# Latent attention in a hybrid decoder trunk: rotated query's products first, values per token in places of their own, latents' scaling with priority

## The chip, the cores and the metric

The kernel runs on one core of a Trainium2 chip. The metric is the device time of one execution in microseconds (us). Engines go by the profile's names: PE is TensorE's matrix multiply, PEld its weight load, DVE is VectorE, ACT is ScalarE, POOL is GpSimd, SP is SyncE, which only issues transfers here. Each engine takes its instructions in the order in which the program has them, and waits at an instruction until the results that it needs are there.

## The reference

Two layers of a decoder trunk, for one sequence of 512 tokens with 1024 channels, in float32. Each layer normalises its input, projects it, and runs three branches side by side: a Mamba-2 state-space branch (SSD), multi-head latent attention (MLA), and a gated DeltaNet. Each branch is projected and gated, their sum goes through an output projection, and a feed-forward block of width 4096 follows. The change touches the MLA branch:

```python
q = (rmsnorm(cq, q_norm_g) @ w_uq).reshape(Bsz, S, H, MLA_NOPE + MLA_ROPE)
q_nope, q_pe = jnp.split(q, [MLA_NOPE], axis=-1)
q_pe = apply_rope(q_pe, cos[:, :, None, :], sin[:, :, None, :])
kv = (rmsnorm(ckv, kv_norm_g) @ w_ukv).reshape(Bsz, S, H, MLA_NOPE + MLA_V)
k_nope, v = jnp.split(kv, [MLA_NOPE], axis=-1)
k_pe = apply_rope(k_rope, cos, sin)
```

Here cq (512 wide) and ckv (256 wide) are the two latents, H is 8 heads, a head has 128 plain and 64 rotated columns for queries and keys and 128 for values. Scores are the sum of the plain and the rotated product, causal, followed by softmax and the product with the values.

## The kernel before

**Precision.** Each float32 product is made of three faster ones: both operands are split into a high part (a copy on ACT, L159 for weights, L256 and L260 for activations) and a low part (a subtraction on DVE, L160, L257, L261), and PE adds high x high, low x high and high x low (L181 to L183). So before PE can use a tile, ACT and then DVE have to pass over it. Weights come through SP's queue into two raw buffers, are split in pieces of 512 columns, and the splits (tiles whi and wlo) go through a ring of buffers: a cast waits until PE is done with the piece that held its buffer.

**Banks.** PE writes to eight accumulation banks of 512 columns. The program takes them from groups: acc (products, four), sm (scores, transposes, short sums, three) and yt (attention outputs, one). A new tile of a group waits for the last reader of the tile that had the bank.

**A layer's order around MLA.** The input projections of cq, ckv and the rotated key columns come first. Function latent then normalises each latent: per block of 128 tokens ACT squares and sums it (L491), DVE and POOL make the reciprocal root (L264 on DVE, a power on POOL, L265), DVE scales the four blocks (L495), PE transposes them (L500), and split_gain (L260 on ACT for the tile cqh or ckh, L261 on DVE for cql or ckl) splits the transposed tile, times the gain. It is called for cq, then for ck.

Then comes a loop over four pairs of heads (hp). For each pair:

- q products (L181 to L183): weights of 512 rows by 384 columns, in two loads of two 128-row tiles each, split at L552 to L555. The 384 columns are three tiles: head 0, head 1 and the rotated columns of both (pp).
- qh and ql of both heads (L568, L569); qp, the scaled copy of pp (L575); its rotation in rope: four transfers on ACT's queue that swap halves (L513), and three DVE passes with the cosine and sine tables (L515 to L517); a swap of the two heads' halves by two more transfers (L580); and copies into qps and qpl, the high and low parts (L584 to L586).
- k products for both heads, split into kh and kl, with a raised priority; then V for both heads, per block of 128 tokens, split into vh and vl (L257 by way of ev).
- for each head: scores per block of 128 tokens (L607 to L612; L610 and L611 are the rotated part), a row maximum (L616, DVE), an exponential (L619, ACT), a reciprocal and a scaling (L620, L621, DVE); transposes of the probabilities (L629), their split (tiles mix and pt), and the product with V (L645 to L647) into yt; its split gives the head's output y.

**Who orders the instructions.** The program text is not the order on the engines. A list scheduler places instructions by their priority, which follows the text unless a block raises it (tc.high_priority), as soon as it estimates that their inputs are ready. It so fills PE's waits with products of the next head pair, and at the end of MLA with the SSD branch's first input projections (w_in weights, tiles acc<-xh,whi), whose convolution (L661 to L665, tile cva) follows on ACT and DVE.

## Time and profile before

| what | value |
|---|---|
| median of 3 runs | 2356.81 us (2356.48 to 2356.88) |
| the profiled execution | 2355.78 us |
| its span, first to last instruction | 2354.0 us |
| granted PE clock | 0.999 |
| busy: PE, DVE, ACT | 98%, 68%, 49% |
| MLA in layer 0 | about 57 to 196 us |
| MLA in layer 1 | about 1224 to 1361 us |

A row of a timeline gives start, length, engine, line, operation, output tile and input tiles, shape, and how many instructions were put together; in square brackets stands how long the engine was idle before the row, and what released it. The view of waits sums such idle times by line and releaser: total, times, longest. A row of the windows view gives a stretch, its length, the busy time of PE, PEld, DVE, ACT and POOL with their instruction counts, then the granted PE clock, the share of the transfer engines and GB/s. The view of transfers gives for each group the queue, the count, the size of one, and the time from issue to landing.

### The profile page before, as it was taken

How to read it: one execution, taken by the hardware profiler on the slowest of the kernel's cores; microseconds unless marked ns; L12 is line 12 of the kernel's file. 1: busy time of each engine (PE TensorE's matmuls, PEld its weight loads, DVE VectorE, ACT ScalarE, POOL GpSimd, SP SyncE). 2: the span in 40 equal slices, each digit the busy share in tenths (PEclk: the TensorE clock that was granted, in tenths of full speed). 3: DMA queues.
4: the chain of work that ended last, by engine and by line, in shares of the span. 5: the costliest groups of instructions: out<-in, count | busy, mean ns of one | idle time of the engine just before them, and what ended most of it. 6: DMA issues, size and time to landing. Idle time of an engine off the chain costs nothing.

```text
span 2354.0 us, 32092 instructions
## 1 busy us (share of the span) xinstructions
PE 2312.0 (98%) x11972; PEld 1901.6 (81%) x11972; DVE 1610.0 (68%) x3184; ACT 1155.4 (49%) x2305; POOL 62.5 (3%) x84
## 2 busy tenths in 40 slices
PE   8999999999999999999999999999999999999998
PEld 7778788888887888888887787888888878888886
DVE  6776756775675468667767767667756645677668
ACT  6655434533454345545656553444335534455545
POOL 0000000000000000000000000000000000000000
PEclk9999999999999999999999999999999999999999
DMA  4222232252222443233132222223422224333231
GB/s 136 85 64 71 70 92 72 76 148 72 72 63 72 138 151 106 72 126 116 44 100 79 72 72 71 91 67 104 117 81 63 63 81 159 128 109 107 90 108 45
DMA packets 194172, 215.16 MB, mean 91 GB/s; under 512 B 32352, under 2 KB 153696, under 8 KB 194016
## 3 DMA queue, kind: packets, MB, share of 16 engines
q1 hardware_dynamic: 190496, 207.87, 27.9%
q10 hardware_dynamic: 3520, 5.25, 0.9%
q8 instruction: 94, 1.54, 0.3%
q14 instruction: 62, 0.51, 0.1%
HBM read 200.50 MB, written 7.34 MB: 88 GB/s over the span
## 4 chain that ended last, share of the span: by engine, by line
PE 81%; issue 9%; DVE 5%; DMA 2%; ACT 1%; POOL 1%; SPq 0%; ACTq 0%; DVEq 0%; POOLq 0%
PE acc L181 20%; PE acc L183 20%; PE acc L182 20%; PE sm L181 2%; PE sm L183 2%; PE sm L182 2%; DVE wlo L160 1%; PE sm L629 1%; PE yt L182 1%; PE yt L183 1%; PE yt L181 1%; PE sm L984 1%; PE sm L724 1%; PE sm L965 1%; DMA mix<-mix 1%
## 5 line engine op out<-in xcount | busy, mean ns | idle before, releaser
L160 DVE TENSOR_TENSOR wlo<-wraw,whi 128x512 fp32r<-128x512 f32 x552 | 378.6, 689 | 399.3 <-ACT whi L159 392.5
L159 ACT CAST whi<-wraw 128x512 fp32r<-128x512 f32 x552 | 342.0, 621 | 628.1 <-PE acc L182 417.2
L181 PE MATMUL acc<-xh,whi 128*128 128x512 f32 (+1 forms) x1184 | 462.2, 391 | 2.2 <-DVE vl L257 2.2
L183 PE MATMUL acc<-xh,wlo 128*128 128x512 f32 (+1 forms) x1184 | 459.3, 388 | 0.0
L182 PE MATMUL acc<-xl,whi 128*128 128x512 f32 (+1 forms) x1184 | 459.0, 388 | 0.0
L181 PEld LDWEIGHTS acc<-xh,whi 128*128 128x128 f32 x1184 | 222.8, 189 | 44.3 <-DVE vl L257 2.8
L182 PEld LDWEIGHTS acc<-xl,whi 128*128 128x128 f32 x1184 | 223.0, 188 | 42.7 <-issue 1.0
L183 PEld LDWEIGHTS acc<-xh,wlo 128*128 128x128 f32 x1184 | 222.9, 188 | 42.1 <-issue 0.5
L181 PE MATMUL acc<-yh,whi 128*128 128x512 f32 x384 | 153.1, 402 | 0.0
L182 PE MATMUL acc<-yl,whi 128*128 128x512 f32 x384 | 152.4, 397 | 0.0
L183 PE MATMUL acc<-yh,wlo 128*128 128x512 f32 x384 | 151.4, 394 | 0.0
L183 PE MATMUL acc<-whi,xl 128*128 128x512 f32 (+1 forms) x384 | 144.1, 376 | 0.0
L181 PE MATMUL acc<-whi,xh 128*128 128x512 f32 (+1 forms) x384 | 143.4, 375 | 0.0
L182 PE MATMUL acc<-wlo,xh 128*128 128x512 f32 (+1 forms) x384 | 143.1, 373 | 0.0
L665 DVE SCALAR_TENSOR_TENSOR cva<-acc,pc,cva 128x511 f32<-128x511 f32 (+2 forms) x168 | 120.2, 743 | 16.7 <-ACT cva L661 9.5
L159 ACT CAST whi<-wr 128x512 fp32r<-128x512 f32 x128 | 79.5, 621 | 68.2 <-PE acc L183 29.0
L183 PE MATMUL acc<-whi,yl 128*128 128x512 f32 x256 | 99.7, 390 | 0.0
L181 PE MATMUL acc<-whi,yh 128*128 128x512 f32 x256 | 99.7, 389 | 0.0
L182 PE MATMUL acc<-wlo,yh 128*128 128x512 f32 x256 | 99.6, 389 | 0.0
L160 DVE TENSOR_TENSOR wlo<-wr,whi 128x512 fp32r<-128x512 f32 x128 | 86.0, 688 | 12.4 <-ACT whi L159 11.7
L181 PEld LDWEIGHTS acc<-yh,whi 128*128 128x128 f32 x384 | 71.6, 188 | 16.9 <-ACT yh L260 2.3
L182 PEld LDWEIGHTS acc<-yl,whi 128*128 128x128 f32 x384 | 72.2, 188 | 16.0 <-issue 1.9
(382 smaller groups left out, 4601.7 us busy)
## 6 DMA issues: line engine op xcount, KB each, us to landing
wraw<-in_w_in_dram SPq DMA_DIRECT2D x148, 512.0 KB, 3.4
wraw<-in_w_up_dram SPq DMA_DIRECT2D x64, 512.0 KB, 3.6
wr<-in_w_down_dram SPq DMA_DIRECT2D x32, 1024.0 KB, 4.9
wraw<-in_w_mla_out_dram SPq DMA_DIRECT2D x16, 512.0 KB, 3.3
wraw<-in_w_ssd_out_dram SPq DMA_DIRECT2D x16, 512.0 KB, 3.3
wraw<-in_w_gdn_out_dram SPq DMA_DIRECT2D x16, 512.0 KB, 3.3
wraw<-in_w_out_dram SPq DMA_DIRECT2D x16, 512.0 KB, 3.5
wraw<-in_mla_w_uq_dram SPq DMA_DIRECT2D x16, 384.0 KB, 3.3
```

Source lines behind the costliest of these rows:

```text
L159: act.copy(hi, raw)
L160: dve.tensor_tensor(lo, raw, f32(hi), ALU.subtract)
L181: pe.matmul(o, ah, bh, start=start, stop=False, skip_group_check=more)
L182: pe.matmul(o, ah, bl, start=False, stop=False, skip_group_check=more)
L183: pe.matmul(o, al, bh, start=False, stop=stop, skip_group_check=more)
L629: pe.transpose(ps[:, n : n + P], pn[t][:, kb * P : (kb + 1) * P], ident)
L665: dve.scalar_tensor_tensor(acc[:, d:], ps[:, : S - d], taps_[3 - d], acc[:, d:], ALU.mult, ALU.add)
L724: pe.matmul(py[:, h * 64 : (h + 1) * 64], e2[h // 4][:, h % 4, :], xd[:, h * 64 : (h + 1) * 64], start=True, stop=True)
L965: pe.matmul(pw[:, h * P : (h + 1) * P], Y[:, h, :], r[:, h * P : (h + 1) * P], start=True, stop=True)
L984: pe.matmul(po[:, h * P : (h + 1) * P], pt_[:, h, :], vn[:, h * P : (h + 1) * P], start=True, stop=True)
```

## The change

Three edits in MLA, in both layers; the arithmetic stays as it is.

1. In latent, squares, reciprocal root and scaling stand in a high-priority block, and the fourth tile's transposes go to a bank of the yt group, not of sm.
2. The q products of a pair go in two rounds of two weight tiles; in each round the rotated columns come first, then head 1, then head 0.
3. The values' tiles lie in places of their own for every other pair: pair 1 in the place that outputs y6 and y7 take later, pair 3 in the places of cq's tiles 0 and 1, pairs 0 and 2 in the two vh and vl buffers. V goes through dense_T with a hook: the products of one token block are finished and split before those of the next, where before all four blocks shared each weight piece and were split at the end. The outputs y are claimed one by one when they are made.

```diff
@@ latent
-            for t in range(T):
-                jk = mk(ml, [P, width], F32, "pn3", 2)
-                act.activation(jk, tok[t], AF.Square, accum_out=ss[:, t : t + 1])
-            rs = mk(sp, [P, T], F32, "lrs")
-            rsq(rs, ss, 1.0 / width, EPS)
-            for t in range(T):
-                dve.tensor_scalar(tok[t], tok[t], rs[:, t : t + 1], None, ALU.mult)
+            with tc.high_priority():
+                for t in range(T):
+                    jk = mk(ml, [P, width], F32, "pn3", 2)
+                    act.activation(jk, tok[t], AF.Square, accum_out=ss[:, t : t + 1])
+                rs = mk(sp, [P, T], F32, "lrs")
+                rsq(rs, ss, 1.0 / width, EPS)
+                for t in range(T):
+                    dve.tensor_scalar(tok[t], tok[t], rs[:, t : t + 1], None, ALU.mult)
...
-                ps = sm_bank()
+                ps = y_bank() if k == 3 else sm_bank()
@@ the loop over head pairs
-        yh, yl = hilo_tags(lp, "y")
+        yh, yl = [None] * KD, [None] * KD
...
-            *pq, pp = dense_F(q_weights(), tiles(384), 512, cqh, cql)
+            pss = [acc_bank() for _ in range(3)]
+            gen = q_weights()
+            for k0 in (0, 2):
+                two = [next(gen) for _ in range(2)]
+                for ps, c in reversed(list(zip(pss, tiles(384)))):
+                    for k, wh, wl in two:
+                        mm3(ps, wh[:, 0, c], wl[:, 0, c], cqh[k], cql[k], k == 0, k == 3)
+            *pq, pp = pss
...
-            vs = [[mk(ml, [P, T, P], F32R, nm, 2) for nm in ("vh", "vl")] for _ in range(2)]
+            vs = []
+            for j in range(2):
+                if hp % 2 == 0:
+                    v2 = [mk(ml, [P, S], F32R, nm, 2) for nm in ("vh", "vl")]
+                elif hp == 1:
+                    v2 = [mk(lp, [P, S], F32R, f"y{e}{6 + j}") for e in "hl"]
+                else:
+                    v2 = [mk(ml, [P, S], F32R, f"cq{e}{j}") for e in "hl"]
+                vs.append([x.rearrange("p (t n) -> p t n", t=T) for x in v2])
...
-            dense_T(wkv, 256, 256, ckh, ckl, ev, lambda w: w.rearrange("p (h n) -> p h n", h=2)[:, :, P:])
+            vcols = lambda w: w.rearrange("p (h n) -> p h n", h=2)[:, :, P:]
+            dense_T(wkv, 256, 256, ckh, ckl, ev, vcols, hook=lambda t: None)
...
                         pe.matmul(o, v_l, th[:, c : c + w], start=False, stop=kb == T - 1)
+                yh[2 * hp + j], yl[2 * hp + j] = (mk(lp, [P, S], F32R, f"y{e}{2 * hp + j}") for e in "hl")
                 split_act(yh[2 * hp + j], yl[2 * hp + j], po)
```

## The prediction

> **What bounds the kernel now.** I read the page first (busy time, chain), then what TensorE (PE) waits for over the whole run, then the timelines of PE, DVE and ACT around each of those waits.

> ```profile
> PE 2312.0 (98%) x11972; PEld 1901.6 (81%) x11972; DVE 1610.0 (68%) x3184; ACT 1155.4 (49%) x2305; POOL 62.5 (3%) x84
> ...
> PE 81%; issue 9%; DVE 5%; DMA 2%; ACT 1%; POOL 1%; SPq 0%; ACTq 0%; DVEq 0%; POOLq 0%
> ```

> PE is busy for 2312.0 of 2354.0 us, and the change neither adds nor removes a matmul. So it can win only PE's idle time inside the two attention stages, and lose by making new idle time there. The view of PE's waits (us in total, times, longest) has these rows of those stages:

> ```profile
> PE acc L181 <- DVE vl L257: 3.6, 4, 1.1
> PE sm L610 <- ACT qps L586: 3.2, 4, 1.4
> ...
> PE sm L500 <- DVE mix L495: 2.0, 2, 1.0
> ...
> PE sm L500 <- DVE cql L261: 1.2, 1, 1.2
> ...
> PE acc L181 <- ACT cqh L260: 0.6, 2, 0.3
> ...
> PE yt L646 <- DVE mix L257: 0.5, 2, 0.2
> ```

> These sum to 11.1 us in 15 waits. A product is shown longer than the distance to its successor:

> ```profile
> 67.10 0.40 PE L182 MATMUL acc<-cql,whi 128*128 128x512 f32 x1
> 67.33 0.40 PE L183 MATMUL acc<-cqh,wlo 128*128 128x512 f32 x1
> ```

> Starts lie 0.23 apart, each lasts 0.40 (0.39 at most other rows), so a shown idle of i costs i + 0.16. The 15 waits cost 11.1 + 2.4 = **13.5 us**: all that can be won, 0.57%. Below, every new wait is counted in the same measure, from the start that PE could have had to the start that it gets, and set against these 13.5.

> **The change part by part.** Both programs' instruction order per engine is known, with what each instruction waits for; only their times are not. DVE, ACT and PE take their instructions in that order, so I put durations of before on the changed order.

> **1. Latents with priority.** PE, then ACT and DVE, layer 0:

> ```profile
> 56.90 1.47 PE L500 MATMUL sm<-ct,mix 128*128 128x128 f32 x12
> 58.67 0.98 PE L181 MATMUL acc<-cqh,whi 128*128 128x512 f32 x3 [0.30 <-ACT cqh L260]
> 60.86 0.66 PE L500 MATMUL sm<-ct,mix 128*128 128x128 f32 x4 [1.21 <-DVE cql L261]
> ...
> 64.79 0.63 PE L500 MATMUL sm<-ct,mix 128*128 128x128 f32 x4 [0.97 <-DVE mix L495]
> ```
> ```profile
> 57.93 1.85 ACT L260 ACTIVATE cqh<-sm,pc 128x512 fp32r<-128x512 f32 x3
> 59.65 0.43 ACT L491 ACTIVATE pn<-mix 128x256 f32<-128x256 f32 x1
> ```
> ```profile
> 59.96 0.19 DVE L415 TENSOR_SCALAR dtq<-spl 128x64 f32<-128x64 f32 x1
> 60.06 2.06 DVE L261 SCALAR_TENSOR_TENSOR cql<-sm,pc,cqh 128x512 fp32r<-128x512 f32 x3
> ...
> 62.94 0.16 DVE L264 TENSOR_SCALAR lrs<-lss 128x4 f32<-128x4 f32 x1
> 64.29 0.62 DVE L495 TENSOR_SCALAR mix<-mix,lrs 128x256 f32<-128x256 f32 x2 [1.19 <-POOL lrs L265]
> ```

> Before, the four cql come first, then ck's lrs, its power on POOL (1.35 us from lrs to the first scaling) and four scalings, 0.31 each. In the changed order lrs and the four scalings stand ahead of the four cql. The scalings wait on POOL, and all cql are queued behind them; the ck transposes wait for cql 0, whose bank they reuse. The fourth cq transposes have a bank of their own, so 16 run at once: 56.90 + 16 x 0.12 = 58.86. ACT does ck's fourth square ahead of cqh 0 (0.5 us), so PE starts the first three products at about 59.25: 0.4 lost. It would reach the ck transposes at 59.93. DVE is full until 60.1 in either kernel; lrs 60.1, scalings from 61.4, cql 0 from 62.65 to 63.4: **3.45 lost**. In layer 1:

> ```profile
> 1225.28 0.96 PE L181 MATMUL acc<-cqh,whi 128*128 128x512 f32 x3 [0.29 <-ACT cqh L260]
> ...
> 1230.01 0.63 PE L500 MATMUL sm<-ct,mix 128*128 128x128 f32 x4 [0.98 <-DVE mix L495]
> ```
> ```profile
> 1224.54 1.84 ACT L260 ACTIVATE cqh<-sm,pc 128x512 fp32r<-128x512 f32 x3
> ```

> DVE is idle there when the square ends, 0.6 behind the old start of cqh 0: lrs 1225.15, scalings from 1226.5, cql 0 done 1228.5, PE ready at 1226.5: 2.0, and 0.4 again. After 0.4 + 3.45 + 0.4 + 2.0 = 6.25, before (0.30 + 1.21 + 0.97 + 0.29 + 0.98) + 5 x 0.16 = 4.55: **+1.7**. Were POOL's 1.35 nothing, the new waits would be 6.25 - 2.7 = 3.55; with as much DVE work more ahead of them as the four scalings are, some 8.

> [...] PE's longest idle time in this trace is at the start:

> ```profile
> 8.98 0.90 PE L296 MATMUL sm<-ct,xr 128*128 128x128 f32 x3 [8.98 <-DVE xr L291]
> ```
> ```profile
> 9.00:12.00 3.00, 2.70 (x12) 2.27 (x12) 1.50 (x4) 2.20 (x7) 0.89 (x2) 1.00 1.01 382
> ```

> After 8.98 us of idle the granted clock (third column from the end) is 1.00 at once. [...]

> **2. Rotated query first, two query tiles last.** ACT, then DVE:

> ```profile
> 70.51 1.28 ACT L568 ACTIVATE qh<-acc 128x512 fp32r<-128x512 f32 x2 [2.24 <-PE acc L183]
> ...
> 72.48 0.59 ACT L256 CAST kh<-acc 128x512 fp32r<-128x512 f32 x1
> ...
> 74.89 0.62 ACT L526 CAST kph<-mix 128x512 fp32r<-128x512 f32 x1
> ...
> 75.42 0.62 ACT L527 CAST kps<-mix 64x512 fp32r<-64x512 f32 x1
> ```
> ```profile
> 73.11 0.69 DVE L257 TENSOR_TENSOR kl<-acc,kh 128x512 fp32r<-128x512 f32 x1
> ```

> Before, qh is made at 70.5, ahead of kh. Now tile 0's last product stands one behind that of the first k tile, and ACT's order is kh, kph, kps, second kh, qh. V's first product reuses the bank of that k tile: kh starts 0.4 behind PE, kl ends about 1.75 behind, PE has five products (1.15) to do: 0.6. The first score waits for qh: five copies 0.53 apart (74.89 to 75.42) and its own length, 3.2 behind that k tile, where PE could be at 2.45: 0.75. **1.35 a layer, +2.7**; nothing if ACT's copies overlap more, 5 if kph's rotation is late as well.

> **3. Values per token, in places of their own.** The four waits on vl (3.6 + 0.64 = 4.2) and the two at the mix row (0.8) go: at the end of the stage nothing waits for vl any more, since the next bank was left by an earlier head pair. What is late next is the same V after head pair 0: its last copies stand behind qh and query weights' copies, about 0.5 a layer. **-4.0**; 0 to 4 could stay.

> **4. The rotation's own waits.** The rows (PE, ACT, and transfers by issue to landing):

> ```profile
> 115.08 0.39 PE L610 MATMUL sm<-kps,qps 128*128 128x256 f32 x1 [0.35 <-ACT qps L586]
> ```
> ```profile
> 141.56 1.26 ACT L584 CAST qps<-mix 64x512 fp32r<-64x512 f32 x2
> ...
> 144.86 0.62 ACT L159 CAST whi<-wraw 128x512 fp32r<-128x512 f32 x1 [0.97 <-DMA wraw<-in_w_in_dram]
> 145.50 0.61 ACT L586 CAST qps<-mix 64x512 fp32r<-64x512 f32 x1
> ```
> ```profile
> mix<-qp ACTq DMA_DIRECT2D x16, 64.0 KB, 2.0
> mix<-mix ACTq DMA_DIRECT2D x8, 128.0 KB, 2.3
> ```

> The four qps waits of before cost 3.2 + 0.64 = 3.85. With pp first the rotation (2.0 + two DVE passes + 2.3) starts earlier, but the copies into qps are queued. Head pair 2 is the clearest: two casts of the next stage's w_in weights stand in front of the four qps copies, and the second waits for a query product six before the rotated scores. With 0.42 from a product's start to its reader, 0.62 and four copies of 0.63: -1.36 + 0.42 + 0.62 + 2.52 = **2.2 late**. The same working gives 0.3 at pair 0, 0.5 at pair 1, none at pair 3, and 0.35 where pair 0's last softmax row comes late. 3.35 a layer, 6.7 against 3.85: **+2.85** (from 2 to 9 for both layers).

> **5. The seam to the state-space stage.** This is not in the edit's lines, but the order moves: the SSD convolution's second two input banks are filled sooner, and the third two are asked for right behind. PE, ACT, DVE in before:

> ```profile
> 197.45 0.39 PE L182 MATMUL acc<-xl,whi 128*128 128x512 f32 x1
> ```
> ```profile
> 197.87 0.62 ACT L159 CAST whi<-wraw 128x512 fp32r<-128x512 f32 x1 [0.83 <-PE acc L182]
> ```
> ```profile
> 198.53 0.69 DVE L160 TENSOR_TENSOR wlo<-wraw,whi 128x512 fp32r<-128x512 f32 x1 [1.11 <-ACT whi L159]
> 199.14 1.40 DVE L665 SCALAR_TENSOR_TENSOR cva<-acc,pc,cva 128x510 f32<-128x510 f32 x2
> ```

> In before, PE has 23 more products to do on the banks that it holds (23 x 0.23 = 5.3 us) while DVE works through wlo and the convolution's last passes. In the changed order the product that frees the weight buffer is the last but one, and the next one needs the bank that the second of these passes reads. From that product: +0.42 cast, +0.66 wlo, +0.61 and 1.40 for the passes = 3.09, of which PE covers two products, 0.45: **2.65 a layer, +5.3** (2 to 3.3 each).

> **The sum.** +1.7 + 2.7 - 4.0 + 2.85 + 5.3 = **+8.55**. The profiled execution took 2355.78 us, the median is 2356.81, 1.03 more: 2355.78 + 8.55 = 2364.3 for such an execution, **2365.4** as a median (+0.36%). With all lower bounds the new waits are 9.6 against 13.5 (2353), with all upper ones 33 (2376).

> **The rivals.** (a) *It does as the edits aim: faster.* One mechanism: ACT and DVE run so far ahead of PE that a late copy is always done when PE asks. Then the waits on vl, qps and mix go (8.85 with their drains), and only the latents' new order and qh remain (4.4): 2356.8 - 8.85 + 4.4 = 2352.4; without those too, 2343.3. It decides at the casts in front of qps: they must end over 2.5 us ahead of the rotated scores. For it: DVE is 68% busy, ACT 49%. Against it: the waits of before already come from such queues (0.97 idle at a cast ahead of qps). I take 2350.
> (b) *No change*: the seam's convolution is ready, say because its weights' cast slips in sooner. Without part 5: 2360.1. That the priority moves nothing would give 2356.8; but the order does move.
> (c) *More idle than counted*: DVE's delays add up behind the latents: 2370 to 2376.
> [...]

> **How the numbers follow.** Forecast (2361.5 to 2368) 0.46; (a) 0.14; (b) 0.18; (c) 0.18; (d) 0.04. A difference of 0.2%, 4.7 us, is about what a measurement of this kernel can tell from no change: below 2352.1 faster, above 2361.5 slower. That is faster 0.14, same 0.18, slower 0.68. The range from 2353 (all lower bounds, which leaves out most of (a)) to 2372 (which leaves out the end of (c)) holds some 8 in 10.

> **What would show it.** In the changed profile: a PE wait on cql of over 3 us in layer 0 and about 2 in layer 1 (part 1); new waits on qh and kl at the first scores and V (2); vl gone from PE's waits, at the stage's end above all (3); rotated scores waiting on qps about 2 us at pair 2 in both layers (4); a wait of some 2.6 us on cva behind the attention in both (5). If cva is not among PE's waits, part 5 falls and the time is near 2360; if qps is not either, (a) holds.

## The result, and the profile after

**2372.20 us** (median of 6 runs, 2370.74 to 2375.02), against 2357.22 for the kernel before (6 runs, 2356.48 to 2359.39): ratio **1.0064** (95% interval 1.0054 to 1.0073), 15.0 us slower. The direction was forecast, the size not: +8.55 was predicted, and the time lies 0.2 us beyond the range's upper end.

The profiled execution of after took 2373.0 us, with a span of 2371.2, so +17.2 on the span of before. The page's first line:

```profile
PE 2318.9 (98%) x11972; PEld 1906.7 (80%) x11972; DVE 1609.0 (68%) x3184; ACT 1157.0 (49%) x2305; POOL 62.5 (3%) x84
```

Against 2312.0 in before, PE was busy 6.9 us longer with the same 11972 instructions. So the loss has two parts: idle time grew by 10.3 us (span less busy: 42.0 to 52.3), and the same products took 6.9 us more. The forecast knew only the first.

Not all of this lies in the attention stages. The windows view from the first transpose of cq to the SSD branch's first product behind the seam (L461), before, then after, layer 0 and layer 1:

```profile
56.90:248.23 191.33, 184.84 (x992) 151.01 (x991) 142.25 (x326) 111.79 (x269) 1.54 (x2) 1.00 0.26 76
1223.52:1413.85 190.33, 184.71 (x993) 151.09 (x991) 139.87 (x316) 111.63 (x268) 1.54 (x2) 1.00 0.25 74
```
```profile
58.50:259.27 200.77, 189.05 (x992) 154.30 (x991) 141.55 (x323) 112.63 (x269) 1.54 (x2) 0.97 0.25 72
1234.26:1430.75 196.49, 186.14 (x992) 152.10 (x991) 139.42 (x315) 112.34 (x268) 1.54 (x2) 0.99 0.25 72
```

After reaches the latents 1.6 us later, 58.50 against 56.90, in a part of the program that no edit touches (the other traces of this kernel's versions reach them at 57.9 or later). The two stages take 9.4 and 6.2 us longer: **15.6** in all, 10.0 of it idle and 5.6 busy.

PE's waits in after (total, times, longest):

```profile
PE sm L629 <- ACT qps L595: 9.3, 6, 2.1
...
PE acc L181 <- DVE cva L685: 5.2, 2, 2.6
PE sm L501 <- DVE cql L261: 4.1, 2, 2.5
...
PE acc L181 <- DVE kl L257: 1.3, 4, 0.5
...
PE sm L626 <- ACT qh L577: 0.6, 2, 0.3
PE acc L181 <- ACT cqh L260: 0.5, 2, 0.2
...
PE sm L626 <- ACT pn L638: 0.2, 1, 0.2
```

These are the attention stages' waits: 21.2 us in 19, where before had 11.1 in 15. vl is gone, as meant, and so is the mix row; qps has grown from 3.2 to 9.3, and cva and cql have 9.3 together where before had 1.2 (cql). In the prediction's measure (0.16 more for each wait) that is 24.2 against 13.5: **+10.7**.

The busy part is in the timeline of PE. In layer 0 the latents' wait is followed by products whose starts lie 0.43 apart, each 0.63 long, and only from 70.1 on by the usual 0.23 and 0.39:

```profile
64.07 1.12 PE L501 MATMUL sm<-ct,mix 128*128 128x128 f32 x4 [2.45 <-DVE cql L261]
...
68.40 0.63 PE L183 MATMUL acc<-cqh,wlo 128*128 128x512 f32 x1
68.83 0.63 PE L181 MATMUL acc<-cqh,whi 128*128 128x512 f32 x1
...
70.81 0.40 PE L182 MATMUL acc<-cql,whi 128*128 128x512 f32 x1
71.04 0.39 PE L183 MATMUL acc<-cqh,wlo 128*128 128x512 f32 x1
```

The view of windows has the granted clock in the third column from the end (after, then before):

```profile
65.00:70.00 5.00, 5.00 (x15) 4.02 (x15) 3.05 (x5) 1.38 (x2) 0.00 (x0) 0.50 0.17 39
...
160.00:165.00 5.00, 5.00 (x30) 4.14 (x30) 4.02 (x13) 3.62 (x12) 0.00 (x0) 0.77 0.00 0
```
```profile
65.00:70.00 5.00, 5.00 (x27) 4.17 (x26) 3.85 (x8) 1.79 (x3) 0.00 (x0) 1.00 0.45 132
```

From 65 to 70 us PE is busy throughout in both, with 15 products at clock 0.50 in after and 27 at 1.00 in before. The column is the mean of the trace's clock record, a list of stretches with the clock granted in each. After's holds three half-speed stretches in the attention stages: 6.83 us from 63.3, 3.41 us from 158.9 and 3.41 us from 1329.6. Before's has none there. (Both records start late, at 18.9 us in after and at 16.4 in before, and both end at half speed with the program, from 2367.3 in after and from 2347.8 in before.) Of the three stretches PE waited for 1.0 us. The other 12.7 us, with starts 0.43 apart in place of 0.23, lose an estimated **5.9**.

So waits and clock make 10.7 + 5.9 = 16.6 where the stages grew by 15.6. The two parts are the right ones to within 1.0; where that goes is not shown.

### The profile page after: what moved, and what is told of

It reads as the page before. It is cut to its first block, busy times and chain, and to the rows that moved or that the text cites. A ratio compares the mean times of both kernels' runs of the same rounds, so it can differ in the third digit from the quotient of the medians.

```text
span 2371.2 us, 32109 instructions
## 1 busy us (share of the span) xinstructions
PE 2318.9 (98%) x11972; PEld 1906.7 (80%) x11972; DVE 1609.0 (68%) x3184; ACT 1157.0 (49%) x2305; POOL 62.5 (3%) x84
## 3 DMA queue, kind: packets, MB, share of 16 engines
q10 hardware_dynamic: 3520, 5.25, 0.8%
## 4 chain that ended last, share of the span: by engine, by line
PE 83%; issue 8%; DVE 5%; DMA 2%; ACT 1%; POOL 1%; SPq 0%; DVEq 0%; POOLq 0%; ACTq 0%
PE acc L181 21%; PE acc L182 21%; PE acc L183 21%; PE sm L181 2%; PE sm L182 2%; PE sm L183 2%; DMA mix<-mix 1%; DVE wlo L160 1%; PE yt L182 1%; PE yt L183 1%; PE yt L181 1%; PE sm L1004 1%; PE sm L648 1%; PE sm L744 1%; PE sm L985 1%
## 5 line engine op out<-in xcount | busy, mean ns | idle before, releaser
L160 DVE TENSOR_TENSOR wlo<-wraw,whi 128x512 fp32r<-128x512 f32 x552 | 378.0, 689 | 408.2 <-ACT whi L159 388.8
L159 ACT CAST whi<-wraw 128x512 fp32r<-128x512 f32 x552 | 341.7, 621 | 630.1 <-PE acc L182 416.0
L181 PE MATMUL acc<-xh,whi 128*128 128x512 f32 (+1 forms) x1184 | 462.4, 392 | 5.2 <-DVE cva L685 5.2
L183 PE MATMUL acc<-xh,wlo 128*128 128x512 f32 (+1 forms) x1184 | 459.7, 389 | 0.0
L182 PE MATMUL acc<-xl,whi 128*128 128x512 f32 (+1 forms) x1184 | 459.5, 388 | 0.0
L181 PEld LDWEIGHTS acc<-xh,whi 128*128 128x128 f32 x1184 | 222.8, 189 | 47.3 <-ACT cm L451 6.0
L182 PEld LDWEIGHTS acc<-xl,whi 128*128 128x128 f32 x1184 | 223.0, 188 | 42.3 <-issue 1.0
L183 PEld LDWEIGHTS acc<-xh,wlo 128*128 128x128 f32 x1184 | 222.9, 188 | 41.8 <-issue 0.5
L181 PE MATMUL acc<-yh,whi 128*128 128x512 f32 x384 | 153.0, 402 | 0.0
L182 PE MATMUL acc<-yl,whi 128*128 128x512 f32 x384 | 152.4, 397 | 0.0
L183 PE MATMUL acc<-yh,wlo 128*128 128x512 f32 x384 | 151.3, 394 | 0.0
L183 PE MATMUL acc<-whi,xl 128*128 128x512 f32 (+1 forms) x384 | 144.1, 376 | 0.0
L181 PE MATMUL acc<-whi,xh 128*128 128x512 f32 (+1 forms) x384 | 143.8, 376 | 0.0
L182 PE MATMUL acc<-wlo,xh 128*128 128x512 f32 (+1 forms) x384 | 143.2, 373 | 0.0
L685 DVE SCALAR_TENSOR_TENSOR cva<-acc,pc,cva 128x511 f32<-128x511 f32 (+2 forms) x168 | 120.1, 742 | 18.9 <-ACT cva L681 9.5
L159 ACT CAST whi<-wr 128x512 fp32r<-128x512 f32 x128 | 79.5, 621 | 68.2 <-PE acc L183 32.7
L183 PE MATMUL acc<-whi,yl 128*128 128x512 f32 x256 | 99.7, 389 | 0.0
L181 PE MATMUL acc<-whi,yh 128*128 128x512 f32 x256 | 99.7, 389 | 0.0
L182 PE MATMUL acc<-wlo,yh 128*128 128x512 f32 x256 | 99.6, 389 | 0.0
L160 DVE TENSOR_TENSOR wlo<-wr,whi 128x512 fp32r<-128x512 f32 x128 | 85.8, 685 | 12.5 <-ACT whi L159 11.9
L182 PEld LDWEIGHTS acc<-yl,whi 128*128 128x128 f32 x384 | 72.2, 188 | 16.0 <-issue 1.9
L181 PEld LDWEIGHTS acc<-yh,whi 128*128 128x128 f32 x384 | 71.6, 188 | 16.7 <-ACT yh L260 2.3
```

The costliest lines, as they stand in the source:

```text
L159: act.copy(hi, raw)
L160: dve.tensor_tensor(lo, raw, f32(hi), ALU.subtract)
L181: pe.matmul(o, ah, bh, start=start, stop=False, skip_group_check=more)
L182: pe.matmul(o, ah, bl, start=False, stop=False, skip_group_check=more)
L183: pe.matmul(o, al, bh, start=False, stop=stop, skip_group_check=more)
L685: dve.scalar_tensor_tensor(acc[:, d:], ps[:, : S - d], taps_[3 - d], acc[:, d:], ALU.mult, ALU.add)
```

## The experiments

"Before" below is the kernel before, run beside each group on the same chip (medians 2357.35, 2356.43 and 2356.92). Ratios stand with their 95% interval. The theory after the result: the waits as the profile shows them, and on top of them a clock that falls after waits of about 2 us. Its rivals: that the rows at half speed are an artefact or come from the edits' products, and that one of the three edits alone carries the loss.

### Each edit alone

**e1_latent**: before with edit 1 only (the first two changes of the diff, in latent).

```diff
+            with tc.high_priority():
+                for t in range(T):
+                    jk = mk(ml, [P, width], F32, "pn3", 2)
...
-                ps = sm_bank()
+                ps = y_bank() if k == 3 else sm_bank()
```

> The first edit alone (squares, root and scaling with priority, fourth tile's transposes in the yt bank). Theory A (the loss is new waits, and on top of them PE at half clock after some of them): the latents' waits are those of the changed kernel, 0.25 + 2.45 us in layer 0 and 0.25 + 1.66 in layer 1, 5.25 with their drains against 4.55 before, so +0.7 from waits; after the 2.45 us wait the granted clock falls to 0.5 for several us, which makes it +3 to +4 in runs where it falls. Theory B (waits alone, the low clock in the changed kernel's profile is chance of that execution): +0.7, clock 0.999. Either way no wait on cva at the seam.

2362.18 us (11 runs), 1.0020 (1.0012 to 1.0029): +4.8. Its waits and its page:

```profile
PE sm L501 <- DVE cql L261: 4.1, 2, 2.5
```
```profile
PE 2315.8 (98%) x11972; PEld 1905.4 (81%) x11972; DVE 1609.3 (68%) x3184; ACT 1155.2 (49%) x2305; POOL 62.5 (3%) x84
```

The latents' waits are after's: with cqh 5.25 against 4.55, +0.7. PE's busy time is up by 3.8, of which 0.9 lies ahead of the latents and 2.7 in layer 0's attention stage, and the clock record has the same 6.83 us at half speed from 63.1. In this trace the two attention stages take 4.0 us longer than in before, inside the measured +2.8 to +6.8; the waits' 0.7 alone is not.

**e2_qorder**: before with edit 2 only (the two rounds of q products).

> The second edit alone (rotated columns first, heads reversed). Both theories: the waits on kl and qh at the first V product and the first score appear (about 1.1 a layer with drains, +2.2); vl's waits stay as before. If the late qps of pair 0 comes from this edit (its swap's transfers meeting the weight loads), the wait of about 1.6 us at pair 0 is here too, +3.4 for both layers: +4 to +6 in all. If it comes from the values' edit, +1 to +3. No wait on cva; no wait over 2 us, so by theory A the clock stays up.

2356.74 us (11 runs), 0.9995 (0.9986 to 1.0004): no difference, where a loss was expected. The new waits are there, two of 1.18 and 1.30 on kl at V:

```profile
PE acc L181 <- DVE vl L257: 2.6, 4, 0.9
PE acc L181 <- DVE kl L257: 2.5, 2, 1.3
...
PE sm L617 <- ACT qps L593: 0.9, 2, 0.7
```

But qps falls from 3.2 to 0.9 and vl from 3.6 to 2.6. So products of pp first do bring the rotation forward, as the edit says; what gives that away in after comes with edit 3.

**e3_values**: before with edit 3 only (places of the values, order of V).

> The third edit alone (values per token in places of their own). Both theories: vl gone from PE's waits (-4 to -5), the wait of 2.6 us on cva at the seam in both layers (+5.5), qps at pair 2 behind casts of w_in weights (up to +2 a layer): 0 to +5. Theory A adds 1.6 us for each pause of over 2 us that is followed by half clock, so up to +9 and a spread of several us between executions; theory B adds none and the spread is that of before.

2365.98 us (5 runs), 1.0035 (1.0023 to 1.0048): +8.6, the largest of the three.

```profile
PE sm L619 <- ACT qps L586: 9.9, 8, 2.7
...
PE acc L181 <- DVE cva L675: 3.9, 2, 2.0
```
```profile
120.00:125.00 5.00, 3.52 (x13) 2.79 (x14) 3.13 (x10) 4.01 (x11) 0.00 (x0) 0.66 0.00 0
```

vl is gone, 4.2 with 0.16 for each of its waits. In its place qps waits 9.9 in 8 waits instead of 3.2 in 4, and the seam's cva is there. The longest qps wait, 2.70 at 118.8 to 121.5, is followed by half speed (0.66 in the row); the clock record has four such windows, one behind each cva wait and each of two qps waits. So edit 3 brings the seam and most of the qps waits. That PE, no longer stopped for vl, comes sooner than ACT's queue is ready is a reading of these waits; no run tests it alone. The three alone add up to 4.8 - 0.6 + 8.6 = 12.8 of the 15.0; the 2.2 between are within what the four intervals leave open (2 to 3 us to each side of each).

### Does a wait set the clock?

**m_pause** leaves the reference's computation out: 160 streams of 30 to 44 equal products, between them pauses made by a chain of 0 to 14 operations on DVE, in random order. The chain's result, times zero, goes into the next stream's operand (gate), so that the stream has to wait for it.

```diff
+        for i in range(m):
+            pe.matmul(acc, w, gate, start=i == 0, stop=i == m - 1)
+        dve.tensor_copy(tmp, acc[:, :256])
+        for _ in range(int(n)):
+            dve.tensor_scalar(tmp, tmp, 0.5, None, ALU.mult)
...
```

> This kernel leaves out the whole computation: it runs 160 streams of 30 to 44 products of 128x512 and makes PE wait between them for a chain of 0 to 14 short DVE operations, in random order; its output is only a copy of the input. Theory A: after pauses below about 1.5 us the next products start 0.23 us apart; above 2 us a growing share of the pauses is followed by 3.4 to 7 us with starts about 0.43 to 0.46 apart (granted clock 0.5), and well above 3.5 us nearly all. Theory B: the clock stays at 1.0 after pauses of any length up to 5 us.

```
full-speed window, idle in it   followed by half speed
0 to 1.75 us                      0 of 333
1.75 to 2.00 us                   4 of  13
2.00 us and more                114 of 114
half-speed window, idle in it   still half speed in the next
under 0.50 us                     0 of 116
0.50 to 0.75 us                   5 of   7
0.75 us and more                 60 of  60
```

The view of windows shows what that does where pauses are dense, 5.31 us busy in ten with a clock of 0.73:

```profile
110.00:120.00 10.00, 5.31 (x15) 3.90 (x14) 4.13 (x13) 0.00 (x0) 0.73 0.00 0
```

So in this run the waits set the clock: here all products are alike, and only the pauses differ. In after the window at the latents had 1.92 us idle (1.67 of the 2.45 and the 0.25 ahead of it) and pair 2's had 2.07 in both layers, and half speed followed; the two waits of 2.61 at the seam lay across two windows each, with at most 1.80 in one, and it did not. An estimate from after's rows is that a half-speed window costs up to 1.6 us (3.41 us with starts 0.43 apart in place of 0.23). Another followed 65 of m_pause's 67 with 0.50 us or more idle in them, and after's one with 0.78. The count of after's full-speed windows agrees: none of 29 windows with 0.25 to 1.75 us idle, one of two with 1.75 to 2.00, and both above. These counts show no sharp edge: half speed also followed one window of e1_latent with 1.72 us idle and one of x_qps with 1.74.

### Where the waits come from

**x_seam**: after, with the first two convolutions of the SSD branch raised in priority.

```diff
-            with tc.high_priority():
+            with tc.high_priority(up):
-                conv(ps, c, which)
+                conv(ps, c, which, 2000 if g == 0 else None)
```

> The changed kernel with the two convolutions at the seam put ahead of the next weights' subtraction on DVE. Theory A (waits, and half clock after a pause that takes more than about 1.9 us of one 3.41 us window): the cva wait of 2.6 us in each layer falls to about 0.9, so -3.4 against the changed kernel from waits, and up to 1.7 more for each half-clock window that these pauses had set off: -3.4 to -6.8 (about 2366 to 2369). Theory B (the waits cost their length, the clock falls at random): -3.4, as many half-clock windows as before. Theory C (the seam's wait is covered elsewhere): no change.

2370.33 us (5 runs), 1.0055 (1.0043 to 1.0068), some 2 us less than after where 3.4 to 6.8 were expected. The two cva waits fall from 5.2 to 2.7, 0.79 and 1.96 in the layers:

```profile
PE acc L181 <- DVE cva L685: 2.7, 2, 2.0
```

Half of the seam is the order on DVE, then. The interval reaches after's, so the total alone shows nothing.

The trace shows something else, which bears on the clock. At the latents PE waits 0.25 and 2.45 us as in after, at the same instructions, but the grid lies a quarter of a microsecond earlier against the wait. No window then has more than 1.67 us idle, and no half speed follows: 26 products from 65 to 70 us where after has 15.

```profile
63.98 0.66 PE L501 MATMUL sm<-ct,mix 128*128 128x128 f32 x4 [2.45 <-DVE cql L261]
```
```profile
65.00:70.00 5.00, 5.00 (x26) 4.19 (x25) 4.32 (x8) 2.72 (x6) 0.00 (x0) 1.00 0.27 66
```

So the same wait of 2.45 us was followed by half speed in after and not here, with another place on the grid, and part of any one execution's time here is chance.

**x_bank**: after without the priority in latent; the fourth bank stays.

```diff
-            with tc.high_priority():
-                for t in range(T):
-                    jk = mk(ml, [P, width], F32, "pn3", 2)
+            for t in range(T):
+                jk = mk(ml, [P, width], F32, "pn3", 2)
...
```

> The changed kernel without the priority on squares, root and scaling; the fourth tile's bank stays. Theory A: the ck transposes now stand behind more products, the wait on cql falls from 2.45 and 1.66 to about 0.6 each (-3), and no half-clock window follows in layer 0 (-3): about -6 against the changed kernel (2366). Theory B: -3 (2369), low clock in layer 0 as likely as before. Theory C (something else in the latents ends last): under -1.

2368.83 us (5 runs), 1.0053 (1.0040 to 1.0065), some 3 us less than after where 6 were expected.

```profile
PE sm L628 <- ACT qps L594: 6.2, 4, 2.1
...
PE acc L181 <- ACT whi L159: 2.3, 2, 1.2
...
PE acc L182 <- DVE cql L261: 1.4, 1, 1.4
```

The 2.45 and its two half-speed windows are gone. Part of the gain goes into 2.3 us of waits on whi, at pair 1's first key products, that after does not have. Both half-speed windows that are left follow pair 2's 2.07.

**f_bank**: before with the bank alone, no priority, edits 2 and 3 not made.

```diff
-                ps = sm_bank()
+                ps = y_bank() if k == 3 else sm_bank()
```

> The kernel before with the fourth tile's bank alone. Both theories: the waits on cqh, cql and mix in the latents, 4.55 us with drains over both layers, become about 2.4; all other waits as before, none over 1.5 us, clock up. -2 against before (about 2355).

2360.46 us (11 runs), 1.0015 (1.0006 to 1.0024): slower, where 2 us of gain were expected. The latents wait as little as in x_bank, but two rotated scores now come too soon:

```profile
PE sm L610 <- ACT qps L586: 5.2, 3, 2.0
```

1.91 and 1.98 at pair 0; of m_pause's windows with 1.75 to 2.00 us idle, 4 of 13 were followed by half speed. The 11 times lie in two groups, 2357.5 to 2358.4 and 2359.8 to 2362.0; the profiled one is of the first and has no half-speed window. That the second has them fits their mean clock (0.997 to 0.998, 0.999 in the first group and in one of the second), but no trace of one was taken.

**f_bank_q**: f_bank with edit 2.

> The bank and the second edit together, on the kernel before. Theory A and B: the sum of f_bank (-2) and of the second edit alone (-0.6): -2 to -3 against before, no pause over 1.5 us, clock up.

2355.46 us (11 runs), 0.9995 (0.9986 to 1.0004). Edit 2 takes f_bank's qps waits away: 5.0 us less than f_bank, from the order of the q products alone. Against before it can't be told from no difference.

**x_dma**: after, with seven eighths of pair 1's key and value weights not loaded but set to zero by POOL, so its keys and values are not the reference's.

```diff
+            if cut > 1:
+                pool.memset(rk[:, :, n // cut :], 0.0)
-            sync.dma_start(raw.rearrange("p (k n) -> p k n", n=n),
+            sync.dma_start(rk[:, :, : n // cut],
...
-            wkv = list(weights(a["mla_w_ukv"][ly], hp * 512, 512, 256))
+            wkv = list(weights(a["mla_w_ukv"][ly], hp * 512, 512, 256, cut=8 if hp == 1 else 1))
```

> The changed kernel, but of the key and value weights of head pair 1 only an eighth of the columns is loaded (64 KB for 512 KB; POOL fills the rest with zeros, so pair 1's keys and values are wrong). In the changed kernel this load is issued 0.6 us behind the two transfers that swap pair 0's rotated halves, and the later of these lands 5.4 us after its issue. Theory A (the transfers share their engines with the weight load): the swap lands within 2.5 us or so, a weights' load of 384 KB still 1.6 us behind it, and the wait on qps at pair 0 falls from 1.55 and 1.61 to under 0.8. Theory B (ACT's queue or the transfer's own length sets it): the wait stays over 1.3.

One run, 2367.25 us. What it asks about is pair 0 in after, where ACT waits for the second of two swap transfers (rows of ACT, then SP's queue, then the transfer's time from issue to landing from 80 to 100 us, shortest, median, longest):

```profile
85.79 1.15 ACTq L589 DMA_DIRECT2D mix<-mix  x2
...
91.70 0.61 ACT L595 CAST qps<-mix 64x512 fp32r<-64x512 f32 x1 [1.61 <-DMA mix<-mix]
```
```profile
86.37 0.37 SPq L172 DMA_DIRECT2D wraw<-in_mla_w_ukv_dram  x1
87.39 0.37 SPq L545 DMA_DIRECT2D wraw<-in_mla_w_uq_dram  x1
```
```profile
DMA to landing us min/median/max: 2.3/3.8/5.4
```

And x_dma, the same transfers (its line L592) and its waits on qps:

```profile
DMA to landing us min/median/max: 2.3/2.5/2.6
```
```profile
PE sm L632 <- ACT qps L598: 2.3, 2, 1.2
```

With most of the load behind it gone, the second transfer lands after 2.6 instead of 5.4 us, and the waits of pairs 0 and 1 go. Only pair 2's two are left, 1.23 and 1.11 where after had 2.07; why they are shorter is not shown. So at pair 0 the wait is the transfer's, which took 5.4 us with that load behind it and 2.6 without most of it, and not ACT's queue. At pair 1 the landing changed as well (4.5 at most in after, 2.3 here), but what runs beside it there was not varied by itself.

### What is left if the waits are treated

**x_qps**: after, with priority 30 on the rotation, the swap and the copies into qps, which all move into the block.

```diff
-            qr = rope(qp)
+            with tc.high_priority(30):
+                qr = rope(qp)
...
```

> The changed kernel with the query's rotation, swap and qps copies at a raised priority: at pairs 1 and 2 no cast of other weights is left in front of the first three qps copies, and as the order moves, the first SSD banks are asked for later, so that nothing waits on cva at the seam. Theory A (waits plus half-clock windows): qps from 10.2 us with drains to under 4, cva 5.5 to nothing, the latents' 2.45 us wait and its half-clock windows stay: -9 to -13 against the changed kernel (2360 to 2364). Theory B (waits alone, clock at random): -11, spread as in the changed kernel. Theory C (the scheduler's other moves eat it): within 4 of the changed kernel.

2369.50 us (5 runs), 1.0051 (1.0038 to 1.0063): some 3 us of the 9 and more expected.

```profile
PE acc L181 <- DVE cql L257: 4.3, 2, 2.2
...
PE acc L181 <- DVE kl L257: 2.3, 2, 1.2
PE sm L630 <- ACT qps L596: 2.3, 1, 2.3
...
PE sm L627 <- ACT qh L577: 1.7, 2, 0.9
```

qps falls from 9.3 to 2.3 and cva goes, but 4.3 appear on cql, which is V of pair 3 in its new place (L257, 2.16 a layer), at the stage's end. kl and qh grow. That the copies that go first have displaced those is likely, but not shown by a run. The latents' 2.45 and 1.66 are as in after, and five half-speed windows remain.

**g_sbq30**: x_qps, x_bank and x_seam together.

> The changed kernel with all three mended: no priority in the latents (the bank stays), the seam's convolutions ahead on DVE, the rotation and qps with raised priority. Theory A: waits in the two attention stages about 9 to 12 us with drains against 13.5 before, no pause that fills 1.9 us of a window, so no half clock but at the very end: 2352 to 2356, spread under 3 us. Theory B: the same waits, half-clock windows now and then: up to 2360. Theory C: over 2360.

2363.61 us (6 runs), 1.0031 (1.0018 to 1.0043), a sure gain on after, but not the 2352 to 2356 expected. The profiled execution has no half-speed window before the program's end, and its page shows PE busy for 2314.0. Its longest waits, 1.89 and 1.87 at pair 2, are of the length at which 4 of 13 windows in m_pause were followed by half speed; two of the other runs have a mean clock of 0.997 against its 0.999, but no trace of them was taken. What is left is idle time, now on qh at the first scores:

```profile
PE sm L626 <- ACT qh L576: 7.2, 8, 1.2
PE sm L629 <- ACT qps L595: 3.8, 2, 1.9
```

**g_bqq30**: before with the bank, edit 2 and x_qps' block; no priority in latent, the values as before.

> The kernel before with the bank, the second edit, and the rotation and qps with raised priority. Theory A and B: as with bank and second edit alone (2355.5), without the one wait of 0.6 us on qps left there: 2354 to 2356; no half clock.

**2354.17 us** (11 runs, 2352.70 to 2355.31), 0.9989 (0.9980 to 0.9998): 2.75 us faster than before, 18 faster than after. The interval ends only 0.5 us from no difference.

```profile
PE sm L618 <- ACT qps L594: 2.1, 4, 1.5
...
PE acc L182 <- DVE cql L261: 1.4, 1, 1.4
```

The longest of the attention stages' waits is 1.53 us, and none lowers the clock; vl is no longer among PE's waits, with the values where they were.

## Why the prediction was wrong in size

The step that failed is in part 1: "After 8.98 us of idle the granted clock (third column from the end) is 1.00 at once." The sum then had no term for the clock, and the numbers left 0.04 to its fall, as (d). In after the clock falls for four windows: an estimated 5.9 us by the spacing of the products.

The row (clock 1.00 in 9.00 to 12.00, after 8.98 us idle) could not carry this, for it measures nothing. Before's clock record starts at 16.4 us, and the column gives 1.00 where nothing is recorded. PE's own rows show the pace there, in before:

```profile
15.93 0.41 PE L182 MATMUL yt<-xl,mix 128*96 128x256 f32 x1
16.14 0.41 PE L183 MATMUL yt<-xh,mix 128*96 128x256 f32 x1
...
16.52 0.28 PE L182 MATMUL yt<-xl,mix 128*96 128x256 f32 x1
16.64 0.28 PE L183 MATMUL yt<-xh,mix 128*96 128x256 f32 x1
```

The same products start 0.21 apart up to 16.4 us and 0.12 apart behind it. So PE did run at half pace behind its longest idle time, and the trace that the prediction read had it. m_pause then has 114 windows with 2 us idle or more, all followed by half speed.

The second step, smaller: part 4's 0.3 at pair 0 and 0.5 at pair 1, which took 2.3 us for the swap's transfer. It needed up to 5.4 beside weight loads that the new order starts right behind it, and 2.6 in x_dma.

```profile
92.37 0.39 PE L629 MATMUL sm<-kps,qps 128*128 128x256 f32 x1 [1.55 <-ACT qps L595]
...
157.52 0.39 PE L629 MATMUL sm<-kps,qps 128*128 128x256 f32 x1 [2.07 <-ACT qps L595]
```

Point by point, in its measure, both layers:

| step | predicted | in the profile of after |
|---|---|---|
| 1, latents | 6.25 (4.55 before) | 5.25: 0.25, 2.45, 0.25, 1.66 |
| 1, the clock there | 0 | 2.8 in layer 0 |
| 2, kl at V and qh at pair 0 | 2.7 | 2.2: kl 0.49 and 0.48, qh 0.30 twice |
| 3, values | 4.0 won, 1.0 left | vl and the mix row gone; 0.64 left, on kl at pair 1 |
| 4, qps | 6.7 (3.85 before) | 10.6: 1.55, 1.22, 2.07, none in layer 0; 1.61, 0.74, 2.07, none in layer 1; 0.35 at a last softmax row |
| 4, the clock behind pair 2 | 0 | 3.1 |
| 5, seam | 5.3 | 5.5: 2.61 twice |

Right, then, was the working from durations on the changed order: it came within 0.5 for parts 2, 3 and 5, within 1.0 for part 1, and within 0.2 for pair 2's copies. By the waits alone the time would have been about 2367.5, inside the range. That the range's end lies only 0.2 us short is no merit of it, since no bound of it held a term for the clock. ACT's rows at pair 2 are as worked out, two casts, the second waiting for a product, and four copies behind:

```profile
154.41 0.62 ACT L159 CAST whi<-wraw 128x512 fp32r<-128x512 f32 x1 [0.75 <-PE acc L182]
154.94 1.25 ACT L593 CAST qps<-mix 64x512 fp32r<-64x512 f32 x2
156.22 1.25 ACT L595 CAST qps<-mix 64x512 fp32r<-64x512 f32 x2
```

Part 5, which is not in the edit's lines, came within 0.2, and e3_values shows that it hangs on edit 3. Of the rivals, (a) and (b) fall: ACT and DVE are not ahead, and the seam is there. (c) gives the right microseconds for a wrong reason, more idle behind the latents; they have less than forecast. A falling clock, to which the numbers give 0.04 as (d), is there: the estimated 5.9.

What stays open: whether the three edits together cost more than alone (the 2.2 us are inside the intervals), and how much of after's spread (2370.7 to 2375.0) is which pauses fall into one window. The wait of 2.45 us differs between after and x_seam by its place on the grid, and half speed followed in after alone; no run here was started at a chosen place of it.

## What to carry to other kernels

Where PE is 98% busy, don't add up its waits alone: look at the clock behind the longest of them. In after four windows of 3.41 us at clock 0.50 stood behind waits of 2.07 and 2.45 us, and took an estimated 5.9 us on top of the waits; behind its 29 full-speed windows with 0.25 to 1.75 us idle the clock stayed at 1.00. Before you trust a clock column, see whether the record covers the stretch; the distance between equal products shows the pace even where it does not (0.21 us and then 0.12 in before, where the column had 1.00 for both).

Removing one wait in a chain of copies mostly moved PE to the next. The version that won, by little (g_bqq30), brought one late chain forward and kept every wait of the attention stages at 1.53 us or less, while the one that freed the values' buffers (e3_values) gained 4 us there and lost more at the copies and the seam.

## What the hardware showed unexpectedly

- In m_pause half speed went with the idle time within one window of 3.41 us: it followed 0 of 333 windows under 1.75 us idle, 4 of 13 from 1.75 to 2.00, and 114 of 114 from 2.00 (and one each in e1_latent and x_qps at 1.72 and 1.74). The length of a wait alone did not decide it: 2.45 us at the latents halved the clock in after and not in x_seam, and in after 2.07 at pair 2 did so in both layers, 2.61 at the seam in neither. Of m_pause's half-speed windows none of the 116 under 0.50 us idle was followed by another, all 60 from 0.75 were.
- A transfer of 128 KB from one tile to another took a median of 2.3 us in before (2.2 to 5.5). At pair 0 of layer 0 in after the slower of two, issued at 85.79 and 86.32 us, took 5.4, with two weight loads issued on another queue at 86.37 and 87.39; in x_dma, with an eighth of the first load, it took 2.6.
